# Wider weight sums in two buffers, a fold with a quarter of its own, and kept weights without padding, in a one-core encoder layer

## The chip, the core and the metric

The kernel runs on one core of a Trainium2 chip. A core has five engines that run side by side: PE multiplies matrices, DVE (VectorE) and ACT (ScalarE) work on elements, POOL (GpSimd) is a slower helper, and SP (SyncE) does nothing here but issue transfers between the chip's main memory (DRAM below) and the on-chip buffers. Each engine runs its own instructions in order. A DMA that SP issues runs on 16 DMA engines by itself; if SP has to wait before it may issue one, all that SP has behind it waits too. The metric is device time in microseconds (us), the median of three runs.

## The reference

One layer of a hybrid encoder on 2048 prompt rows and 64 sample rows of width 1024, in float32:

```
h    = rmsnorm(x, g1) * (1 + sc1) + sh1
u, q, k, v, o, gates = split(h @ w_in)
pool_out = (causal window means of u - u) @ w_pool * s_pool        # 4 channel groups
hs   = mlstm(q, k, v, gates)                                      # 4 heads, chunks, state C, n, m
x    = x + gt1 * (concat(pool_out, norm(hs) * sigmoid(o)) @ w_out)
h2   = rmsnorm(x, g2) * (1 + sc2) + sh2
a, g = split(causal_conv3(h2 @ w_up))
x    = x + gt2 * ((silu(g) * a) @ w_down)
```

The shifts, scales and gates (sh, sc, gt) are `c_act @ w_ada + b_ada`, with one vector for the prompt and one for the sample.

## The kernel before, in words

**Arithmetic.** Every float32 product is made of three matmuls on split numbers: a weight piece is loaded (tile `raw`, L390), ACT writes its high part (L411), DVE its low part (L414), and PE multiplies high by high, high by low and low by high. The same split pieces serve more than one group of rows, so after the first split they are kept in DRAM (`hl_kept`, stored by L419) and read back whole (L395) by later groups.

**Stages.** The attention part goes over four groups of rows (group 0 to 3, to about 793 us of the profile), then the feed-forward part over three groups of 704 rows. In the attention part the large products are L477 and the small ones of the recurrent heads are L1282 to L1361; `GL` holds the decay factors of a head, `kw` its weighted keys, `at` its attention scores, `st` its states after each chunk. The feed-forward products are L1572 (up) and L2015, L2138 (down); their moving operand is `hx`, made by L768 from normalised rows that were written to DRAM (`h2d`) and are loaded again (`fscr`, L802).

**Side work.** Work that isn't on the main line runs as generators: each `yield` ends a step, and the main program calls for a step of each waiting generator from time to time (`bg` lists, `drain` finishes them). Three matter here.
- `ada` (L177) makes one modulation vector out of 16 loads of `w_ada`. In group 0 the loads go to a tile with tag "w4"; DVE sums them (L208, L210), and L220 adds up over partitions.
- `fold` (L874) folds the pooling weights into the output weights: it loads two 128-row pieces of `w_out` (L878), multiplies each by `WPT` on PE (L885), lets ACT write the result over the piece, and stores it to `wo_in` (L889). Four such pairs, in group 0.
- `up_sums` (L844) prepares the feed-forward part, where the up-projection is done with sums of weight blocks: it loads the four blocks of a tile, makes four sums or differences on DVE (L863 to L867) and stores them to `wsum` (L872). It begins with group 1, and the feed-forward part loads `wsum` in place of plain weights.

**Buffers.** The tag "w4" has four buffers of [128, 4, 256], taken in turn by `ada`, `fold` and `up_sums`. The tiles of the feed-forward part, `fscr` among them, are laid over room that the attention part gives up at its end.

**Order.** The order on each engine comes out of a list scheduler that goes by data, buffers and priorities; some instructions of the side work are pinned to the order in which they are written.

## Time and profile before

| | us |
|---|---|
| median of three runs | 2185.01 (2181.26 to 2185.93) |
| span of the profiled execution | 2178.0 |
| PE busy | 2155.1 (99%) |
| DVE busy | 1631.7 (75%) |
| ACT busy | 1093.7 (50%) |
| sums of up-projection weights on DVE | from 229.5 to 758.4 |
| loads of `w_out` for the fold | from 76.7 to 112.8 |
| stores of the fold | from 92.3 to 129.3 |

The profiled execution is one run with its own time: what the profiler calls the span is 2178.0 us, and the table's first row is measured around whole runs. A row of the timeline has its start, its duration, engine, line, operation, tiles and shape, and in brackets the idle time of the engine just before it with what ended that idle time. "SPq" rows are issues: the transfer itself lands some microseconds later.

### The profile page before, as it was taken

The page shows a single profiled execution, that of the slowest core. Times are in us where ns is not written, and L with a number is a line of the kernel's source. Part 1 is how long each engine was busy: PE and PEld are TensorE (multiplying, and loading weights), DVE is VectorE, ACT ScalarE, POOL GpSimd, SP SyncE. Part 2 cuts the span into 40 slices and gives each one's busy share as a digit, 9 for nine tenths or more (in the row PEclk, how much of TensorE's full clock was granted, in tenths as well). Part 3 has the DMA queues.
Part 4 walks back from the last instruction along what each step waited for, and adds up shares of the span by engine and source line. Part 5 has one row for each costly group of instructions (what it writes and reads, how often), then busy time and mean ns, then how long its engine had stood idle before and what let it go on. Part 6 is the DMA issues. An engine that isn't in the chain of part 4 may idle for free.

```text
span 2178.0 us, 38112 instructions
## 1 busy us (share of the span) xinstructions
PE 2155.1 (99%) x13553; PEld 2041.6 (94%) x13553; DVE 1631.7 (75%) x3040; ACT 1093.7 (50%) x2181; POOL 241.6 (11%) x474
## 2 busy tenths in 40 slices
PE   8999999999999999999999999999999999999998
PEld 7888888888899999999999999999999999999998
DVE  5868668757955678797967668888886587887874
ACT  4554335234333456474736445655655364565554
POOL 0010000001000101010101121100101331111112
PEclk9999999999999999999999999999999999999999
DMA  8886997988879387788967966666668675555542
GB/s 325 327 297 226 312 312 259 310 291 273 296 263 305 130 279 255 267 306 295 349 211 257 316 244 225 237 201 215 227 220 275 217 255 183 170 179 190 172 161 81
DMA packets 297351, 539.51 MB, mean 248 GB/s; under 512 B 25760, under 2 KB 114336, under 8 KB 297160
## 3 DMA queue, kind: packets, MB, share of 16 engines
q1 hardware_dynamic: 287720, 514.75, 69.8%
q10 hardware_dynamic: 9440, 22.32, 2.6%
q8 instruction: 107, 1.75, 0.3%
q14 instruction: 84, 0.69, 0.1%
HBM read 410.98 MB, written 125.98 MB: 247 GB/s over the span
## 4 chain that ended last, share of the span: by engine, by line
PE 82%; DMA 7%; DVE 7%; issue 2%; ACT 1%; SPq 1%; POOL 0%; DVEq 0%; POOLq 0%; ACTq 0%
PE mm L1572 35%; PE mm L477 19%; PE mm L2138 12%; PE mm L2015 8%; PE mm L1117 2%; DVE wt L414 2%; DMA raw<-w_ada 1%; DMA wt<-wsum 1%; DMA hl_kept<-wt 1%; DMA wsum<-w 1%; PE m L1307 1%; PE m L1329 1%; PE m L1327 1%; PE m L1292 1%; DVE scr L250 1%
## 5 line engine op out<-in xcount | busy, mean ns | idle before, releaser
L1572 PE MATMUL mm<-hx,wt 128*128 128x352 f32 x5544 | 887.0, 321 | 3.7 <-DVE hx L768 1.9
L1572 PEld LDWEIGHTS mm<-hx,wt 128*128 128x128 f32 x5544 | 878.6, 188 | 6.8 <-DVE hx L768 2.8
L477 PE MATMUL mm<-hl,wt 128*128 128x512 f32 (+2 forms) x1920 | 386.2, 357 | 0.2 <-ACT va L250 0.2
L411 ACT ACTIVATE wt<-raw 128x512 fp32r<-128x512 f32 (+3 forms) x470 | 276.8, 597 | 185.2 <-PE mm L477 63.5
L477 PEld LDWEIGHTS mm<-hl,wt 128*128 128x128 f32 x1920 | 315.4, 189 | 48.2 <-issue 5.3
L414 DVE TENSOR_TENSOR wt<-raw,wt 128x512 fp32r<-128x512 f32 (+3 forms) x470 | 312.2, 670 | 53.2 <-ACT wt L411 52.7
L2138 PE MATMUL mm<-av,wt 128*128 128x448 f32 (+1 forms) x1632 | 262.7, 322 | 0.0
L2138 PEld LDWEIGHTS mm<-av,wt 128*128 128x128 f32 x1632 | 250.4, 188 | 11.1
L1987 DVE SCALAR_TENSOR_TENSOR x<-mm,MOD,x 128x352 f32<-128x352 f32 (+3 forms) x360 | 167.2, 503 | 79.2 <-PE mm L2138 65.7
L2015 PE MATMUL mm<-av,wt 128*128 128x352 f32 x1344 | 220.6, 323 | 1.8 <-DVE x L1987 0.7
L2015 PEld LDWEIGHTS mm<-av,wt 128*128 128x128 f32 x1344 | 215.4, 188 | 4.8 <-DVE ea L1581 2.8
L1619 ACT ACTIVATE mm<-mm 128x352 f32<-128x352 f32 x196 | 87.8, 448 | 240.0 <-PE mm L1572 184.0
L477 PE MATMUL mm<-mx,wt 128*128 128x512 f32 (+1 forms) x960 | 182.6, 352 | 0.0
L477 PEld LDWEIGHTS mm<-mx,wt 128*128 128x128 f32 x960 | 159.3, 188 | 22.5
L1550 DVE SCALAR_TENSOR_TENSOR ta<-ea,V,ta 128x704 f32<-128x704 f32 (+1 forms) x132 | 125.6, 952 | 63.2 <-ACT ta L1545 51.2
L1550 DVE SCALAR_TENSOR_TENSOR tg<-eg,V,tg 128x704 f32<-128x704 f32 (+1 forms) x132 | 125.7, 952 | 61.0 <-ACT tg L1545 58.5
L414 DVE TENSOR_TENSOR wt<-wt 128x512 fp32r<-128x512 f32 x196 | 132.7, 683 | 12.8 <-ACT wt L411 12.7
L411 ACT ACTIVATE wt<-wt 128x512 fp32r<-128x512 f32 x196 | 119.2, 622 | 43.1 <-DMA wt<-wsum 40.1
L1759 ACT ACTIVATE tg<-tg 128x704 f32<-128x704 f32 (+1 forms) x66 | 52.5, 795 | 70.5 <-DVE tg L1550 70.5
L1528 POOL COPY ea<-UC 128x2 f32<-128x2 f32 x66 | 32.8, 497 | 482.6 <-DVE ta L1550 394.0
L1117 PE MATMUL mm<-wt,hl 128*128 128x256 f32 (+1 forms) x576 | 71.3, 284 | 0.0
L1117 PEld LDWEIGHTS mm<-wt,hl 128*128 128x128 f32 x576 | 70.4, 190 | 0.8 <-issue 0.6
(304 smaller groups left out, 2188.2 us busy)
## 6 DMA issues: line engine op xcount, KB each, us to landing
wt<-wsplit SPq DMA_DIRECT2D x132, 512.0 KB, 4.2
raw<-w_up SPq DMA_DIRECT2D x198, 256.0 KB, 3.8
wt<-hl_kept SPq DMA_DIRECT2D x96, 512.0 KB, 6.0
wt<-wsum SPq DMA_DIRECT2D x132, 256.0 KB, 5.3
wsplit<-wt SPq DMA_DIRECT2D x66, 512.0 KB, 5.5
w<-w_up SPq DMA_DIRECT2D x88, 256.0 KB, 3.7
wsum<-w SPq DMA_DIRECT2D x44, 512.0 KB, 4.9
Bd<-fscr ACTq DMA_DIRECT2D x56, 352.0 KB, 4.3
```

The source lines that it names most:

```text
L411: act.activation(u.w[:, 0, :u.n], u.raw[:, :u.n], AF.Copy)
L414: dve.tensor_tensor(out=u.w[:, 1, :u.n], in0=u.raw[:, :u.n], in1=u.w[:, 0, :u.n].bitcast(F32), op=ALU.subtract)
L477: pe.matmul(ps[bi][:, :hi - lo], U[:, a, k % 4 * P:(k % 4 + 1) * P], mv[k][:, b, lo:hi], start=(at == 0 and pi == 0), stop=(k == order[-1] ...
L1117: pe.matmul(ps[ti][:n, :cols], h[4 * kh + k4][:, b, lo:lo + n], U[:, a, k4 % 2 * cols:(k4 % 2 + 1) * cols], start=(kh == 0 and k4 == 0 and ...
L1528: pool.tensor_copy(ext[:, 0:2], UC[:, f, :])
L1550: dve.scalar_tensor_tensor(out=t[:, :E], in0=ext[:, j:j + E], scalar=wc(j, f), in1=t[:, :E], op0=ALU.mult, op1=ALU.add)
L1572: pe.matmul(bk.t[:, :FH], U[:, a, kc * P:(kc + 1) * P], Bo.at(nm, kc, b), start=(first and kc == 0 and pi == 0), stop=(kc == 3 and pi == 2 ...
L1619: act.activation(to.t[:, :FH], bk.t[:, :FH], AF.Copy)
L1759: act.activation(self.tg[:, :E], self.tg[:, :E], AF.Silu)
L1987: dve.scalar_tensor_tensor(out=x3[n][:, a:b], in0=bk.t[:, a - lo:b - lo], scalar=gt2(n, s), in1=x3[n][:, a:b], op0=ALU.mult, op1=ALU.add)
L2015: pe.matmul(bk.t[:, :FH], U[:, a, c:c + P], quad.put(op, m, b), start=(first and m == 0 and pi == 0), stop=(m == 1 and pi == 2), skip_grou ...
L2138: pe.matmul(bks[i].t[:, :hi - lo], U[:, a, k % 4 * P:(k % 4 + 1) * P], av[k][:, b, lo:hi], start=(k == 0 and (a, b) == PASSES[0]), stop=(k ...
```

## The change

It has three parts.

1. `up_sums` becomes `weight_sums`. A tile is now [128, 4, 512], there are two buffers instead of four, and 22 tiles instead of 44. A load fetches whole rows of 4 KB (before: two runs of 1 KB), and a store is one DMA of 1 MB. There are 44 loads instead of 88, 22 stores instead of 44, and 88 DVE operations on 512 columns instead of 176 on 256. A tile takes seven steps; before, each half tile took four. The new function also has a branch for sums of the down-projection's weights (`dsum`), but its list holds only the up-projection's 22 tiles, so that branch never runs and those sums are made where they were before.
2. In group 0 the two buffers of tag "w4" are cut into four quarters. `ada` goes round three of them, and `fold` has the fourth alone for all of its four pairs, with one more step after each store. A load of the fold can so be issued only when the store before it has read the quarter out and landed.
3. `hl_kept` is [32, 128, 2, 512] instead of [32, 128, 2, 528], so the two halves of a row lie side by side: a store or load moves rows of 4 KB instead of two pieces of 2 KB.

```
-    hl_kept = dr.tile([32, P, 2, WN], F32, tag="hl_kept", name="hl_kept")
+    hl_kept = dr.tile([32, P, 2, 512], F32, tag="hl_kept", name="hl_kept")
...
-        def up_sums():
-            def load(f, c):
-                w = a1.tile([P, 4, 256], F32, tag="w4", name="w4", bufs=4)
-                for i in range(2):
-                    tc.keep_in_program_order(nc.sync.dma_start(out=w[:, 2 * i:2 * i + 2, :], in_=w_up[NF * i + f].rearrange(
-                        "p (h c) -> p h c", h=2)[:, :, c:c + 256]))
-                return w
-            todo = [(f, c) for f in range(NF) for c in (0, 256)]
...
+        def weight_sums():
+            pin = tc.keep_in_program_order
+            todo = list(range(NF))
+            def load():
+                if not todo:
+                    return None
+                f = todo.pop(0)
+                w = a1.tile([P, 4, 512], F32, tag="w4", name="w4", bufs=2)
+                if f < NF:
+                    for i in range(2):
+                        pin(nc.sync.dma_start(out=w[:, 2 * i:2 * i + 2], in_=w_up[NF * i + f].rearrange("p (h c) -> p h c", h=2)))
+                else:
+                    pin(nc.sync.dma_start(out=w, in_=w_quad[f - NF]))
+                return (wsum[f] if f < NF else dsum[f - NF]), w
+            nx = [load(), load()]
+            for _ in range(4):
+                yield
+            while nx[0]:
+                to, w = nx.pop(0)
+                a11, a12, a21, a22 = (w[:, i] for i in range(4))
+                pin(dve.tensor_tensor(out=a22, in0=a21, in1=a22, op=ALU.add))
+                pin(dve.tensor_tensor(out=a21, in0=a11, in1=a21, op=ALU.subtract))
+                yield
+                pin(dve.tensor_tensor(out=a11, in0=a22, in1=a11, op=ALU.subtract))
+                yield
+                pin(dve.tensor_tensor(out=a12, in0=a12, in1=a11, op=ALU.subtract))
+                pin(nc.sync.dma_start(out=to, in_=w))
+                yield
+                yield
+                nx.append(load())
+                yield
+                yield
+                yield
+        quarters = []
+        def quarter(last=False):
+            if not quarters:
+                for _ in range(2):
+                    t = a1.tile([P, 4, 512], F32, tag="w4", name="w4", bufs=2)
+                    quarters.extend([t[:, 0:2], t[:, 2:4]])
+            if last:
+                return quarters[3]
+            quarters.insert(2, quarters.pop(0))
+            return quarters[2]
         def fold():
             for n in range(0, KD, 2):
-                w = a1.tile([P, 4, 256], F32, tag="w4", name="w4", bufs=4).rearrange("p (a b) c -> p a (b c)", a=2)
+                w = quarter(True)
...
                 nc.sync.dma_start(out=wo_in[n:n + 2].rearrange("n p c -> p n c"), in_=w)
+                yield
```

The scheduler and the buffers move instructions beyond what these lines say. Three places follow. A row has the line, the operation, the tile written and the tile read (with the number of the buffer's use), the shape, and "x3" for as many equal rows. Lines from 844 on carry numbers higher by about 20 in the changed kernel.

**The fold in group 0, on SP.** Before, from the second load of `w_out` on (`w_998` and `w_1077` are the first two pairs, `w_1090` a buffer of `ada`):

```order
L878 DMA w_1077<-w_out 128x2x512
L191 DMA w_1090<-w_ada 128x512 x2
L889 DMA wo_in<-w_998 128x2x512
L390 DMA raw<-w_qkou 128x512
L419 DMA hl_kept<-wt 256x1x512
```

In the changed kernel, where `w_758` is the tile whose last quarter is the fold's:

```order
L908 DMA wo_in<-w_758 128x2x512
L191 DMA w_757<-w_ada 128x512 x4
L390 DMA raw<-w_qkou 128x512
L419 DMA hl_kept<-wt 128x1024
L897 DMA w_758<-w_out 128x2x512
L390 DMA raw<-w_qkou 128x512
```

The second load stood ahead of the first store; it now stands behind that store, four loads of `ada` and one weight piece.

**The same on PE.** Before, around the third pair's first half (`m_1273`), and then around the last half of the fourth pair (`m_1504`):

```order
L477 MATMUL mm<-hl_474,wt 128x512 x3
L477 MATMUL mm<-hl_475,wt 128x512 x2
L885 MATMUL m_1273<-w_1223,WPT 128x128 x4
L477 MATMUL mm<-hl_475,wt 128x512
L477 MATMUL mm<-hl_574,wt 128x512 x3
```

```order
L1327 MATMUL m_1485<-st_1447,q 128x129
L1329 MATMUL m_1485<-va,at 128x129
L885 MATMUL m_1504<-w_1434,WPT 128x128 x4
L220 MATMUL m_1511<-u,ones_r 32x512
L220 MATMUL m_1511<-s_778,ones_r 32x512
L220 MATMUL m_1511<-s_1086,ones_r 32x512
L220 MATMUL m_1511<-acc,ones_r 32x512
L477 MATMUL mm<-hl_575,wt 128x512 x3
```

In the changed kernel, around the second pair's first half (`m_1202`), and then around the fourth pair (`m_1581`, `m_1587`):

```order
L477 MATMUL mm<-hl_381,wt 128x512 x3
L477 MATMUL mm<-hl_474,wt 128x512 x2
L904 MATMUL m_1202<-w_758,WPT 128x128 x4
L1347 MATMUL m_1229<-SP_184,q 128x129
L1349 MATMUL m_1229<-va,at 128x129
L1347 MATMUL m_1229<-st_1193,q 128x129
L477 MATMUL mm<-hl_474,wt 128x512
```

```order
L477 MATMUL mm<-hl_475,wt 128x512 x3
L477 MATMUL mm<-hl_574,wt 128x512 x3
L477 MATMUL mm<-hl_575,wt 128x512 x3
L904 MATMUL m_1581<-w_758,WPT 128x128 x4
L904 MATMUL m_1587<-w_758,WPT 128x128 x4
L220 MATMUL m_1594<-u,ones_r 32x512
L220 MATMUL m_1594<-s_778,ones_r 32x512
L220 MATMUL m_1594<-s_1079,ones_r 32x512
```

The second pair went back to about where the third began. The fourth went behind 17 rows of three L477 each, from `hl_575` to the next but one `hl_575`, which before stood behind L220.

**Group 3, the decay factors and states of a head, on DVE.** Before, with sums of three buffers:

```order
L867 TENSOR_TENSOR w_6153<-w_6153 128x256
L863 TENSOR_TENSOR w_6595<-w_6595 128x256
L864 TENSOR_TENSOR w_6595<-w_6595 128x256
L866 TENSOR_TENSOR w_6595<-w_6595 128x256
L867 TENSOR_TENSOR w_6595<-w_6595 128x256
L250 COPY GL<-m_6621 128x20
L250 TENSOR_TENSOR at<-at,mask 128x512
L250 TENSOR_TENSOR at<-at,mask 64x64
L250 TENSOR_TENSOR kw<-m_6670,CL 128x512
L250 TENSOR_TENSOR kw<-m_6676,CL 64x128
```

In the changed kernel, first around the copy of GL, then from behind `kw` on:

```order
L871 TENSOR_TENSOR w_5882<-w_5882 128x512
L714 TENSOR_TENSOR scr<-scr 128x352
L250 COPY GL<-m_6496 128x20
L250 TENSOR_TENSOR at<-at,mask 128x512
L250 TENSOR_TENSOR at<-at,mask 64x64
L250 TENSOR_TENSOR kw<-m_6543,CL 128x512
L250 TENSOR_TENSOR kw<-m_6549,CL 64x128
```

```order
L866 TENSOR_TENSOR w_6326<-w_6326 128x512
L867 TENSOR_TENSOR w_6326<-w_6326 128x512
L250 TENSOR_TENSOR at<-at,m_6581 128x512
L250 TENSOR_TENSOR at<-at,m_6587 64x64
L869 TENSOR_TENSOR w_6326<-w_6326 128x512
L866 TENSOR_TENSOR w_6471<-w_6471 128x512
L867 TENSOR_TENSOR w_6471<-w_6471 128x512
L250 SCALAR_TENSOR_TENSOR st_6611<-SP_185,GL,m_6607 128x129
L869 TENSOR_TENSOR w_6471<-w_6471 128x512
L250 SCALAR_TENSOR_TENSOR st_6613<-st_6611,GL,m_6607 128x129
L871 TENSOR_TENSOR w_6471<-w_6471 128x512
L250 SCALAR_TENSOR_TENSOR st_6615<-st_6613,GL,m_6607 128x129
```

Four sums on `w_6595` that stood right ahead of GL are gone from there. Sums of two tiles, `w_6326` and `w_6471`, stand behind `kw`, and two of the second tile's stand between the state steps.

**The end of the attention part, on SP.** Before:

```order
L640 DMA x2d<-scr 128x576
L872 DMA wsum<-w_7382 512x1x256
L872 DMA wsum<-w_7516 512x1x256
L594 DMA scr<-xT 128x576
L390 DMA raw<-wo_in 128x512
L390 DMA raw<-w_up 128x512
L802 DMA fscr<-h2d 128x704 x4
L640 DMA x2d<-scr 128x576
```

In the changed kernel:

```order
L1441 DMA o_pool<-PO 128x120
L594 DMA scr<-xT 128x576
L390 DMA raw<-wo_in 128x512
L802 DMA fscr<-h2d 128x704 x4
L390 DMA raw<-w_out 128x512
L390 DMA raw<-wo_in 128x512
L640 DMA x2d<-scr 128x576
```

The last two stores of sums stood six and five rows ahead of the first loads of `fscr`. The last store of sums now stands 20 rows ahead of these loads, which stand behind a `scr<-xT` and one weight piece.

More of the change, by code (lines that the diff above doesn't have):

```diff
@@ L194, in load @@
                 nc.sync.dma_start(out=got[i], in_=src[i])
-        lead = 4 if first else 3
+        lead = 4 if quarter else 3
         for i in range(lead):
@@ L872, in up_sums @@
-                pin(nc.sync.dma_start(out=wsum[f, :, :, c:c + 256], in_=w))
+                yield
[9 more added lines that the diff above has]
+            return quarters[2]
```

24 lines of the change are left out of this document (6 added, 18 removed).

## The prediction

> **What bounds the kernel now.** I read the page first, then the table of busy time by stretch, then the tensor engine's timeline wherever a stretch of the touched part has idle time in it. From the page: the span, the tensor engine's row, and the engines' shares of the chain that ended last.
>
> ```profile
> span 2178.0 us, 38112 instructions
> ...
> PE 2155.1 (99%) x13553; PEld 2041.6 (94%) x13553; DVE 1631.7 (75%) x3040; ACT 1093.7 (50%) x2181; POOL 241.6 (11%) x474
> ...
> PE 82%; DMA 7%; DVE 7%; issue 2%; ACT 1%; SPq 1%; POOL 0%; DVEq 0%; POOLq 0%; ACTq 0%
> ```
>
> PE is idle for 2178.0 - 2155.1 = 22.9 us. The change removes no matmul, so a gain can only come out of that idle time, and a loss is a new wait of PE. By stretch (start and end in us, length, then busy time and count of PE, PEld, DVE, ACT, POOL, the granted clock, DMA share, GB/s):
>
> ```profile
> 50.00:100.00 50.00, 48.65 (x265) 40.53 (x264) 40.05 (x74) 28.96 (x66) 1.01 (x1) 1.00 0.88 316
> 100.00:150.00 50.00, 49.50 (x283) 40.80 (x282) 32.33 (x68) 26.36 (x67) 3.98 (x4) 1.00 0.95 347
> 600.00:650.00 50.00, 48.97 (x369) 47.42 (x369) 28.15 (x75) 18.48 (x55) 2.82 (x3) 1.00 0.79 259
> 650.00:700.00 50.00, 50.00 (x368) 45.99 (x367) 31.04 (x87) 21.45 (x70) 3.16 (x6) 1.00 0.94 307
> 793.00:804.00 11.00, 9.00 (x52) 7.84 (x51) 9.85 (x22) 6.36 (x14) 0.00 (x0) 1.00 0.58 199
> ```
>
> In 650 to 700 the transfers run at a share of 0.94 and PE is busy for all 50.00 us: it does not starve beside full DMA engines. Idle time is 1.35, 0.50, 1.03 and 2.00 us in the other four. The timeline of PE names these waits (idle time and its releaser in brackets):
>
> ```profile
> 78.16 1.13 PE L1307 MATMUL m<-va,kw 128*128 128x129 f32 x8 [1.35 <-DVE kw L250]
> ...
> 143.60 0.30 PE L538 MATMUL m<-V,scr 128*128 128x128 f32 x1 [0.50 <-DVE scr L533]
> ...
> 630.19 0.30 PE L1282 MATMUL m<-V,k 128*64 128x128 f32 x1 [1.03 <-DVE GL L250]
> ...
> 795.92 0.59 PE L1572 MATMUL mm<-hx,wt 128*128 128x352 f32 x2 [0.61 <-DVE hx L768]
> ...
> 799.07 2.49 PE L1572 MATMUL mm<-hx,wt 128*128 128x352 f32 x12 [0.82 <-DVE hx L768]
> ...
> 802.08 2.17 PE L1572 MATMUL mm<-hx,wt 128*128 128x352 f32 x12 [0.52 <-DVE hx L768]
> ```
>
> All six end on VectorE, none on a weight that is late. Together they are 4.83 us, and that is about all that this change can win.
>
> **Part 1: the weight sums.** Groups of the tile w, and from the page a VectorE addition on 512 columns:
>
> ```profile
> L863 DVE TENSOR_TENSOR w<-w x44: 404/417/426, 229.5 to 756.1; 128x256 f32<-128x256 f32 x44
> ...
> L867 DVE TENSOR_TENSOR w<-w x44: 405/418/427, 233.3 to 758.0; 128x256 f32<-128x256 f32 x44
> ```
>
> ```profile
> L414 DVE TENSOR_TENSOR wt<-wt 128x512 fp32r<-128x512 f32 x196 | 132.7, 683 | 12.8 <-ACT wt L411 12.7
> ```
>
> Before: 4 lines x 44 x 0.418 = 73.6 us of VectorE. After: 88 x 0.683 = 60.1 us. These 13.5 us are hidden: VectorE is busy for 31.04 of 50 us in the fullest stretch of the sums. Against it, one operation is 0.683 instead of 0.418 long, so a piece that PE waits for may come up to 0.27 us later behind it. PE waited for VectorE three times in the attention part, so bounds are 0 and 3 x 0.27 = 0.8; I take +0.2. The transfers move the same bytes in half as many issues; PE does not wait for them, so 0. Where the moved order matters is shown by two places.
>
> *The last group's decay factors (GL).* VectorE, PE and the issuing queue SP there:
>
> ```profile
> 622.05 0.42 DVE L867 TENSOR_TENSOR w<-w 128x256 f32<-128x256 f32 x1
> 628.25 0.42 DVE L863 TENSOR_TENSOR w<-w 128x256 f32<-128x256 f32 x1 [5.77 <-DMA w<-w_up]
> ...
> 629.97 0.17 DVE L250 COPY GL<-m 128x20 f32<-128x20 f32 x1
> ```
>
> ```profile
> 623.60 1.20 SPq L849 DMA_DIRECT2D w<-w_up  x2
> ```
>
> VectorE stands for 5.77 us before a weight load that was issued at 623.60, does four sums from 628.25, and only then copies GL, for which PE waits 1.03 us at 630.19. In the new order no sum with a pending load stands between the copy and what precedes it, so this wait goes: -1.0 (bounds 0 and -1.03). What is late next: the sums on w_6326 and w_6471 now stand behind kw and ahead of the state sums (st). Each of these loads waits for a store of the tile before it. Store and load cost, and what PE does with st:
>
> ```profile
> wt<-wsplit SPq DMA_DIRECT2D x132, 512.0 KB, 4.2
> ...
> wt<-hl_kept SPq DMA_DIRECT2D x96, 512.0 KB, 6.0
> ...
> w<-w_up SPq DMA_DIRECT2D x88, 256.0 KB, 3.7
> wsum<-w SPq DMA_DIRECT2D x44, 512.0 KB, 4.9
> ```
>
> ```profile
> 639.20 0.39 PE L1327 MATMUL m<-st,q 128*128 128x129 f32 x2
> ```
>
> The last sum of w_5882 ends near 622.5 as in the row at 622.05. SP issues its store between 622.5 and 625.5; it lands 4.9 to 6.8 us later, and the load 3.7 to 4.9 later again: between 631 and 637. PE takes st at 639.20, 638.2 once the 1.03 us are gone. Behind the load stand two sums, the first state step (some 0.4 us), a sum, and the next step: about 3 us to the second step, which PE takes 0.45 us after the first. So the load may land up to about 635.5 before PE waits: 0 to +1.8, taken +0.3 since most of the interval is free.
>
> *The start of the feed-forward part.* SP there, and the last of VectorE's hx:
>
> ```profile
> 743.87 0.43 SPq L594 DMA_DIRECT2D scr<-xT  x1
> ...
> 756.61 2.37 SPq L872 DMA_DIRECT2D wsum<-w  x2
> ...
> 763.91 1.74 SPq L802 DMA_DIRECT2D fscr<-h2d  x4
> ```
>
> ```profile
> 801.08 1.38 DVE L768 TENSOR_TENSOR hx<-fscr,hx 128x352 fp32r<-128x352 f32 x3
> ```
>
> The first loads of the normalised rows (fscr) use room that the weight sums' last stores at 756.61 free, and start at 763.91; what follows ends with hx at 801.08, and PE waits 0.61 + 0.82 + 0.52 = 1.95 us there (2.00 in the table). After, with 7 steps per tile instead of 8 per pair of half tiles, the last store stands 20 rows ahead of these loads, and the loads stand right behind the load scr<-xT that was issued at 743.87. They can start more than 10 us sooner; hx was late by under 1 us at a time. So -2.0 (bounds 0, if hx waits for VectorE's queue and not for its rows, and -2.0).
>
> **Part 2: the fold alone in one quarter.** Before, its four loads rotate over four buffers. After, each load waits until the preceding store from the same quarter has landed, and holds up what SP has behind it; between a store and the next load SP issues a few other DMAs (one, three and two weight pieces). Rows: the load's and the store's time to landing, the first store, the folds on PE, the last store, and what PE does behind the last fold.
>
> ```profile
> w<-w_out SPq DMA_DIRECT2D x4, 512.0 KB, 7.5
> ```
>
> ```profile
> DMA to landing us min/median/max: 6.8/6.8/6.8
> ```
>
> ```profile
> 92.30 0.38 SPq L889 DMA_DIRECT2D wo_in<-w  x1
> ...
> 129.29 0.38 SPq L889 DMA_DIRECT2D wo_in<-w  x1
> ```
>
> ```profile
> 107.97 1.05 PE L885 MATMUL m<-w,WPT 128*128 128x128 f32 x8
> ...
> 124.21 1.05 PE L885 MATMUL m<-w,WPT 128*128 128x128 f32 x8
> ...
> 127.58 1.06 PE L885 MATMUL m<-w,WPT 128*128 128x128 f32 x8
> ...
> 129.56 11.86 PE L477 MATMUL mm<-hl,wt 128*128 128x512 f32 x51
> ```
>
> A store follows the second half of its fold by 129.29 - 127.58 = 1.7 us. PE's new order has fold 2 just ahead of the old place of fold 3 (107.97), without the two halves of the old fold 2 ahead of it (about 0.85 us each) and three matmuls earlier (0.23 each): PE comes to it at 105.5. Fold 3 begins one matmul behind the old place of fold 4 (124.21), with one fold less ahead: 122.7. Fold 4 stands behind the 51 matmuls (0.23 each), which end at 141.4, less one fold and the four small ones that now stand behind it (129.56 - 127.58 - 0.85 = 1.1): 138.6. The second halves of folds 2 and 3 stand at 107.97 less one half and 127.58 less two, so the stores of folds 1, 2 and 3 are issued at 92.3, 108.8 and 127.6. PE covers store plus load up to 13.2, 13.9 and 11.0 us. By the rows they take 6.8 + 7.5 = 14.3: waits of 1.1, 0.4 and 3.3, in all +4.8. But those 7.5 us were measured with SP issuing without a stop; after a wait for a store the queue is nearly empty, and the nearest row for a load of 512 KB is then 4.2: 11.0 in all, and nothing waits. I take a load between (5.5): only fold 4 waits, 12.3 - 11.0 = +1.3. Bounds 0 and +4.8. What queues behind it on PE is everything; on SP the weight loads wait too, but their matmuls are those that PE runs as cover.
>
> The Trainium skill's fixed-cost rule (DMA: Bandwidth & Descriptors, Anatomy of one DMA — SWDGE (gpsimd) path: about 2.0 us plus bytes over 436 GB/s) would make 512 KB an estimated 3.2 us, store and load 6.4, and the fold's term 0, so a sum lower by 1.3; the rows of this trace are longer throughout, on another issue path, and I go by them.
>
> **Part 3: kept split weights without padding.** Stores and loads become whole rows. The nearest rows are wsplit (whole rows, 4.2) and hl_kept (padded, 6.0): up to 1.8 us sooner per load. No wait of PE above ends on such a load, so 0; the cover is that they are issued well ahead, as 650 to 700 shows.
>
> **Sum** against the profiled time: -2.0 - 1.0 + 0.3 + 0.2 + 1.3 = -1.2 us on the span of 2178.0. That span is 7.0 us below the median of 2185.01; the difference lies outside the program and is carried over: 2183.8 us.
>
> **Rivals.** (a) *More waits go*: VectorE's 13.5 us and the shorter transfers also remove the waits at 78.16 and 143.60, and the fold is free: -2.0 - 1.0 - 1.85 = -4.85, 2180.2. For it: both end on VectorE. Against: the sums are not yet running there, so VectorE's work is the same. (b) *Slower: the fold's one quarter becomes a chain* of store, load, matmul. It decides from 13.2, 13.9 and 11.0 us on. At 14.3 it costs 4.8; each further us costs three, since all three are then over: 15.3 gives +7.8. With only half of the gains (-1.5) and the other losses (+0.5): +6.8, 2191.8. For it: a DMA share of 0.95 in 100 to 150; against: SP's own wait empties the queue. The Trainium skill (Trainium Kernel Development and Optimization, Best Practices) asks for double buffers so that DMA overlaps compute, which speaks for this rival; no row of before shows the fold with one. (c) *Nothing moves*: hx is late by VectorE's own queue, GL by another operation, and the fold is covered: 2185.0. That the diff's sums of the down weights run is excluded: its list holds the 22 up-projection tiles only.
>
> **How the numbers follow.** Forecast 0.50, (a) 0.15, (b) 0.22, (c) 0.13. This kernel's runs can tell about 0.2% from no change, 4.4 us. Faster by more needs all of (a), or a good part of it and the spread of the medians: 0.16. Slower by more comes from (b) without its weakest part, and a sliver of the rest: 0.20. Same: 0.64. The range goes from (a), less 1.2 for the spread of single runs (2181.26 to 2185.93), to (b): 2179.0 to 2191.8. The forecast's own range is 2181.5 to 2187.
>
> **What would show it.** Right: no idle time of PE at 793 to 804, none before the GL matmul; at the fold PE waits once, before its fourth tile, for w<-w_out. Wrong: waits of over 1 us on w<-w_out at two or three folds (b); idle time left at the feed-forward start with fscr landed early (c); a wait of PE on st in the last group, which would be the two buffers' price mis-sized; or a changed duration of one L477 or L1572 matmul, which nothing here foresees.

## The result: about 7 us less

The changed kernel takes 2176.43 us (median of six runs, 2172.94 to 2180.3) beside 2184.27 for the kernel before (2181.26 to 2188.65). The ratio is 0.9968, 95% interval 0.9956 to 0.9980, and in a second comparison 0.9971 (0.9958 to 0.9985). Forecast were 2183.8 us in a range of 2179.0 to 2191.8: the sign was right, the size far too small, and the time lies below the range.

From the page of the changed kernel, span, PE, and the shares of the chain that ended last:

```profile
span 2172.8 us, 37945 instructions
...
PE 2154.3 (99%) x13553; PEld 2043.0 (94%) x13553; DVE 1624.5 (75%) x2952; ACT 1094.8 (50%) x2181; POOL 244.7 (11%) x474
...
PE 91%; DVE 3%; DMA 3%; issue 1%; ACT 1%; POOL 0%; SPq 0%; DVEq 0%; POOLq 0%; ACTq 0%
```

PE is idle for 18.5 us instead of 22.9. By stretch, in the same five as before:

```profile
50.00:100.00 50.00, 48.37 (x254) 39.77 (x254) 39.52 (x72) 28.13 (x65) 1.01 (x1) 1.00 0.90 310
100.00:150.00 50.00, 50.00 (x294) 41.79 (x293) 33.04 (x70) 27.03 (x68) 4.02 (x4) 1.00 0.91 336
600.00:650.00 50.00, 50.00 (x378) 48.69 (x377) 30.77 (x71) 20.16 (x59) 2.93 (x3) 1.00 0.82 293
650.00:700.00 50.00, 50.00 (x368) 45.99 (x367) 24.12 (x67) 19.92 (x66) 3.75 (x6) 1.00 0.69 228
793.00:804.00 11.00, 11.00 (x68) 11.00 (x67) 4.79 (x9) 5.66 (x11) 0.00 (x0) 1.00 0.73 239
```

The waits at 143.6, at GL near 630 and at the feed-forward start are gone. The one at 78 stays, and a small one of 0.28 us near 95.6 is new. The sums end early: the last store of a sum is issued at 671.24, and the first loads of `fscr` at 743.93 instead of 763.91.

```profile
671.24 0.32 SPq L872 DMA_DIRECT2D wsum<-w  x1
...
743.93 1.75 SPq L802 DMA_DIRECT2D fscr<-h2d  x4
```

The fold: SP's issues and PE's arrival for the second and the fourth pair, and then the landing times as far as the profile has them, of two of the four stores and of the third pair's load:

```profile
93.24 0.38 SPq L908 DMA_DIRECT2D wo_in<-w  x1
...
97.04 0.38 SPq L897 DMA_DIRECT2D w<-w_out  x1
...
128.46 0.38 SPq L908 DMA_DIRECT2D wo_in<-w  x1
...
132.01 0.44 SPq L897 DMA_DIRECT2D w<-w_out  x1
```

```profile
105.45 1.05 PE L904 MATMUL m<-w,WPT 128*128 128x128 f32 x8
...
138.93 1.95 PE L904 MATMUL m<-w,WPT 128*128 128x128 f32 x16
```

```profile
DMA to landing us min/median/max: 3.0/3.0/3.0
...
DMA to landing us min/median/max: 6.2/6.2/6.2
```

No row of the fold waits for its load. The load for the fourth pair is issued at 132.01, 3.6 us behind the store; if it takes the 6.2 us of the third pair's, it is there at an estimated 138.2, and PE comes at 138.93.

The first profiles of the two kernels differ by 5.2 us, the medians by 7.8. Why these two numbers differ has to be explained too, and so further executions of both kernels were profiled. The expectations below name their theories by letters: **A**, the gain is waits of PE on VectorE that are gone, through the order of instructions; **B**, wide transfers make PE's stream as a whole faster; later **C**, PE has two paces; **D**, VectorE stands before late loads, with PE behind it; and **E**, the wait at GL is usually longer than the first profile shows.

### The profile page after: what moved, and what is told of

Read it like the earlier page. It is cut to its first block, busy times and chain, and to the rows that moved or that the text cites. A ratio compares the mean times of both kernels' runs of the same rounds, so it can differ in the third digit from the quotient of the medians.

```text
span 2172.8 us, 37945 instructions
## 1 busy us (share of the span) xinstructions
PE 2154.3 (99%) x13553; PEld 2043.0 (94%) x13553; DVE 1624.5 (75%) x2952; ACT 1094.8 (50%) x2181; POOL 244.7 (11%) x474
## 4 chain that ended last, share of the span: by engine, by line
PE 91%; DVE 3%; DMA 3%; issue 1%; ACT 1%; POOL 0%; SPq 0%; DVEq 0%; POOLq 0%; ACTq 0%
PE mm L1592 37%; PE mm L477 24%; PE mm L2158 12%; PE mm L2035 9%; PE mm L1137 3%; DVE wt L414 1%; DMA hl_kept<-wt 1%; PE m L1327 1%; PE m L1349 1%; PE m L1347 1%; PE m L1312 1%; DMA wt<-wsum 1%; DMA wt<-dsum 0%; PE mm L1074 0%; PE m L1302 0%
## 5 line engine op out<-in xcount | busy, mean ns | idle before, releaser
L477 PE MATMUL mm<-hl,wt 128*128 128x512 f32 (+2 forms) x1920 | 386.8, 357 | 0.1
L477 PEld LDWEIGHTS mm<-hl,wt 128*128 128x128 f32 x1920 | 315.4, 189 | 48.1 <-issue 5.3
L477 PE MATMUL mm<-mx,wt 128*128 128x512 f32 (+1 forms) x960 | 183.0, 352 | 0.3 <-DVE scr L250 0.3
L477 PEld LDWEIGHTS mm<-mx,wt 128*128 128x128 f32 x960 | 159.4, 188 | 23.1 <-PE mm L477 0.5
(304 smaller groups left out, 2180.3 us busy)
```

Of the source, the lines that this page charges most:

```text
L477: pe.matmul(ps[bi][:, :hi - lo], U[:, a, k % 4 * P:(k % 4 + 1) * P], mv[k][:, b, lo:hi], start=(at == 0 and pi == 0), stop=(k == order[-1] ...
```

## Experiments

### The change again, and its parts alone

**The change itself, second profile.** No edit.

> The changed kernel as it is, beside the kernel before on one chip. The two profiled spans differ by 5.2 us (2178.0 and 2172.8), the medians by 7.8 us. Theory A (order): the gain is the waits of PE on VectorE that are gone (630, 795 to 802, 143.6, 260.6, and some later ones), so 4 to 6 us. Rival B (transfers): longer packets make PE's stream as a whole faster, which one pair of profiles may not show; then 7 us or more, with PE busy time lower by more than 2 us.

Ratio 0.9971 (0.9958 to 0.9985), span 2173.7. PE is busy for 2154.5 us, much as in the first profile of the change, and idle for 19.2. The places are those of theory A. Busy time is only 0.6 us below that of the kernel before, where B asked for more than 2. That the medians differ by 6 to 8 us remains open at this point.

**Part 1 alone: the weight sums.** The fold and `ada` go round all four quarters:

```
-            if last:
-                return quarters[3]
-            quarters.insert(2, quarters.pop(0))
-            return quarters[2]
+            quarters.append(quarters.pop(0))
+            return quarters[3]
```

`hl_kept` keeps 528 columns, and the step after the fold's store, which belongs to part 2, is left out. In this order a quarter can be filled again before the fold has used it, so the folded half of the output weights is not the reference's; instructions and bytes are those of the others.

> Only part 1: weight sums 512 columns wide in two buffers; ada and fold go round all four quarters as before, and kept rows stay padded. Theory A: waits at GL near 630 (1.03 us) and at the feed-forward start (1.95 us) are gone, the one at 143.6 (0.50 us) stays: -3 to -4 us against before. Rival B: since the sums move most of the packets that got longer, nearly the whole gain, -5 us or more.

0.9976 (0.9966 to 0.9986), 5.2 us less by the ratio and 4.6 by the medians, which lies between the two forecasts: most of the gain. GL and the feed-forward start have no wait. Nor is there one at 78 or at 143.6, where A expected the latter to stay. Against it stands one at the fold, where PE comes 6.4 us after the load's issue at 98.59 (the kernel before has 0 to 0.80 us at this place, see below):

```profile
106.99 1.13 PE L902 MATMUL m<-w,WPT 128*128 128x128 f32 x8 [2.00 <-DMA w<-w_out]
```

**Part 2 alone: the fold's own buffer.** Four buffers of [128, 4, 256] as before, the fourth for the fold only, and the step after the store; sums as before.

```
...
+            if not quarters:
+                for _ in range(4):
+                    t = a1.tile([P, 4, 256], F32, tag="w4", name="w4", bufs=4)
+                    quarters.append(t.rearrange("p (a b) c -> p a (b c)", a=2))
+            if last:
+                return quarters[3]
+            quarters.insert(2, quarters.pop(0))
+            return quarters[2]
...
```

> Only part 2: the fold has one buffer of four alone, ada goes round the other three, one more step after the store; sums and kept rows as before. Theory A: the folds' new places move ACT's and PE's work so that the wait at 143.6 goes (-0.5 to -0.7 us), with a new wait of under 0.5 us near 95; the waits at 630 and 795 to 802 stay: 0 to -1 us in all. The prediction's step (fold 4 waits for its load) says +1.3 us.

1.0007 (0.9996 to 1.0017): nothing. The fold doesn't wait for a load, and the wait at 143.6 is gone, but GL and hx are late as ever, GL by more than in any execution of the kernel before:

```profile
634.64 0.30 PE L1296 MATMUL m<-V,k 128*64 128x128 f32 x1 [2.85 <-DVE GL L250]
```

**Part 3 alone: kept weights without padding.** In the kernel before:

```
-    hl_kept = dr.tile([32, P, 2, WN], F32, tag="hl_kept", name="hl_kept")
+    hl_kept = dr.tile([32, P, 2, 512], F32, tag="hl_kept", name="hl_kept")
```

> Only part 3: kept split weights as whole rows; instruction order equal to before. Theory A: loads wt<-hl_kept land in about 4.5 instead of 6.0 us, PE waits where it waited before: 0 us (within 0.5). Rival B: -2 us or more.

1.0004 (0.9993 to 1.0016): nothing. The loads don't even land sooner, where 4.5 us had been expected: 6.0 us before, 6.0 here, and in the change:

```profile
wt<-hl_kept SPq DMA_DIRECT2D x96, 512.0 KB, 5.9
```

**The change without part 3.** The same line the other way round, in the changed kernel.

> The changed kernel with the third part undone: kept split weights padded again (528 columns), everything else and the order of all engines as in the change. Alone this part gave 1.0004 of the time before. Theory A: PE waits for no kept weight, so within 1 us of the changed kernel, 0.9965 to 0.9980 of before. Rival D: kept loads of 562 instead of 327 ns of issue on SP delay the weight-sum loads behind them, VectorE waits for these and PE for VectorE: +2 us or more against the change, with a wait on st near 638.

0.9978 (0.9967 to 0.9990): as the change, within the intervals. No wait on `st`. So the gain belongs to part 1; parts 2 and 3, each by itself, can't be told from nothing.

### What in the weight sums does it

**Eight steps per tile instead of seven.**

```
                 nx.append(load())
                 yield
                 yield
                 yield
+                yield
```

> The changed kernel with eight steps per weight-sum tile instead of seven: the last store of a sum stands 4 rows ahead of the first loads of fscr on SP, as before the change (20 with it); no sum stands ahead of GL. Theory A (order): PE's waits on hx at 795 to 802 come back, +1.5 to +2.5 us against the changed kernel, so -4 to -5 us against before. Rival B (wide transfers): those waits stay away, since 22 long stores are done sooner than 44 short ones; -6 to -7 us.

0.9974 (0.9964 to 0.9984), as the change. The last store comes late again and holds the loads of `fscr` back, as the prediction has it, yet PE loses only 0.52 us:

```profile
754.59 1.08 SPq L872 DMA_DIRECT2D wsum<-w  x1
...
760.83 1.75 SPq L802 DMA_DIRECT2D fscr<-h2d  x4
```

```profile
798.27 4.93 PE L1593 MATMUL mm<-hx,wt 128*128 128x352 f32 x28 [0.52 <-DVE hx L768]
```

They start at 760.83 instead of 763.91, but the main line is 2.3 us sooner here too: PE's first matmul on `hx` is at 791.24 instead of 793.49. Counted back from that matmul, the last of the eight loads is issued 9.8 us ahead here, 7.6 to 8.5 us ahead in the four executions of the kernel before, and 24.7 in the change; PE waits for 0.52, 1.34 to 2.70, and 0 us. So the wait goes with this lead, and a lead longer by 1 to 2 us was worth most of it; why these were won with the store back in its place is not shown. Neither theory's time for this run fitted.

This kernel also has the old pace of the sums: 22 tiles of eight steps are as many steps as 44 half tiles of four. So the gain isn't the pace.

**Short rows.** The transfers of the sums in two column halves:

```
-                        pin(nc.sync.dma_start(out=w[:, 2 * i:2 * i + 2], in_=w_up[NF * i + f].rearrange("p (h c) -> p h c", h=2)))
+                        for c in (0, 256):
+                            pin(nc.sync.dma_start(out=w[:, 2 * i:2 * i + 2, c:c + 256], in_=w_up[NF * i + f].rearrange("p (h c) -> p h c", h=2)[:, :, c:c + 256]))
...
-                pin(nc.sync.dma_start(out=to, in_=w))
+                for c in (0, 256):
+                    pin(nc.sync.dma_start(out=to[:, :, c:c + 256], in_=w[:, :, c:c + 256]))
```

> The changed kernel with each load and store of the weight sums cut into two column halves: as many DMAs, and the same short runs of 1 KB, as before the change; VectorE's operations and the steps stay those of the change. Theory A: order and width of VectorE's operations decide, so within 1 us of the changed kernel, -6 to -7 us against before. Rival B (packets): most of the gain goes, -3 us or less.

1.0037 (1.0023 to 1.0051): 8 us more than before by the ratio, 9.5 by the medians, and some 14 more than the change. Theory A as it stood falls with this: order and width on VectorE are those of the change. But it isn't B's way either. The profiled span is 13.4 us above the mean of the change's three (below): 8.6 in idle time of PE, and 4.8 in busy time, which two stretches at half clock behind its longest waits explain (last section). The two longest:

```profile
285.25 2.09 PE L1329 MATMUL m<-va,kw 128*128 128x129 f32 x8 [2.39 <-DVE kw L250]
...
648.97 0.49 PE L1349 MATMUL m<-st,q 128*128 128x129 f32 x2 [3.93 <-DVE st L250]
```

The second is the place that the prediction named as "what is late next". VectorE's first sum of the tile in question, and SP's issues of its load, here and then in the change:

```profile
647.24 0.69 DVE L867 TENSOR_TENSOR w<-w 128x512 f32<-128x512 f32 x1 [7.14 <-DMA wt<-hl_kept]
```

```profile
639.26 3.12 SPq L857 DMA_DIRECT2D w<-w_up  x4
```

```profile
629.07 0.81 SPq L856 DMA_DIRECT2D w<-w_up  x2
```

The profile puts the 7.14 us down to another load, but the last issue of the tile's own, at 641.77, landed 5.3 us later, just ahead of this sum. Counted from the copy of GL (632.42 here, 625.12 in the change), VectorE begins the tile 14.8 instead of 8.9 us later, and the state steps stand behind it. The first wait, at 285.25, comes behind loads of the modulation weights: VectorE stands for 3.19 and 2.69 us before `raw<-w_ada` at 264.20 and 272.73, and from 275.1 on it has work without a gap up to `kw`.

SP's issues of the sums' loads over the whole kernel, here and in the change (duration of one in ns: least, median, most):

```profile
L857 SPq DMA_DIRECT2D w<-w_up x88: 539/606/1502, 216.6 to 659.2; - x88
```

```profile
L856 SPq DMA_DIRECT2D w<-w_up x44: 328/424/1202, 216.9 to 642.0; - x44
```

Four issues of 0.606 us per tile instead of two of 0.424 keep SP for 2.4 instead of 0.8 us, with two stores of the same kind ahead. The run changes the length of the rows and the number of issues together, so these two aren't told apart. That two buffers leave no room for the longer issues is argued: no run has short rows with another number of buffers.

**Three steps per half tile in the kernel before.**

```
                 w = nx.pop(0)
                 yield
-                yield
```

> The kernel before with one step fewer per half tile (three instead of four) and nothing else: half tiles, four buffers, short rows. The last store of a sum stands 33 rows ahead of the loads of fscr, and no sum that waits for a load stands ahead of GL in group 3. Theory A: the waits at 630 and at 795 to 802 go, those at 78 and 143.6 stay: -3 to -5 us. Rival B: 0 to -1 us.

1.0039 (1.0024 to 1.0053), 9 us more instead of 3 to 5 less. The waits at GL and at the feed-forward start are gone as foreseen. But VectorE now waits seven times for loads of the sums, 14.6 us in all (8.7 in three before), and 40.0 instead of some 30 us for loads of modulation weights. PE waits behind it in groups 1 and 2. The longest of these waits, and what VectorE stood before just ahead of it, a modulation weight:

```profile
  DMA w<-w_up: 14.6, 7
```

```profile
454.53 0.49 PE L1328 MATMUL m<-va,at 128*128 128x129 f32 x2 [3.02 <-DVE at L250]
```

```profile
451.86 0.75 DVE L210 SCALAR_TENSOR_TENSOR s<-raw,CA,s 128x512 f32<-128x512 f32 x1 [4.63 <-DMA raw<-w_ada]
```

**Six steps per tile in the change.**

```
                 nx.append(load())
                 yield
                 yield
-                yield
```

> The changed kernel with six steps per weight-sum tile instead of seven (eight gave 0.9974, seven 0.9971 of before): the next load is asked for as long after the store as before, but its sums come one step sooner. Theory D (VectorE stands before late loads, and PE behind it): waits of VectorE on w<-w_up grow from 1.2 us to 5 or more, PE waits on kw, at, st in groups 1 to 3 for 2 to 8 us in all, 0.998 to 1.002 of before. Rival (only the two places of the prediction count): same as the change.

1.0000 (0.9989 to 1.0011): one step of seven takes the whole gain back, as theory D has it. VectorE's waits on the sums' loads are 8.9 us. PE's longest wait behind 50 us is for `kw`, and right behind it stands one for a kept weight that hadn't landed; VectorE's row shows that ahead of GL and `kw` it stood before a modulation weight:

```profile
440.02 0.91 PE L1326 MATMUL m<-va,kw 128*128 128x129 f32 x6 [2.10 <-DVE kw L250]
...
442.49 2.93 PE L477 MATMUL mm<-hl,wt 128*128 128x512 f32 x6 [1.20 <-DMA wt<-hl_kept]
```

```profile
437.78 0.75 DVE L210 SCALAR_TENSOR_TENSOR s<-raw,CA,s 128x512 f32<-128x512 f32 x1 [4.73 <-DMA raw<-w_ada]
```

The four runs together, beside all executions of the two kernels and part 1 alone (us; VectorE's waits from 200 us on, added up over the timeline; the last column is SP's time in issues of the sums' loads and stores):

| | time ratio | PE idle | VectorE waits for `w_up` | for `w_ada` | SP |
|---|---|---|---|---|---|
| before, four executions | 1 | 22.9 to 24.9 | 8.6 to 9.2 | 28.8 to 31.4 | 78 to 80 |
| change, three executions | 0.9968, 0.9971 | 18.5 to 20.2 | 1.2 to 4.8 | 11.4 to 14.5 | 28 to 29 |
| part 1 alone | 0.9976 | 21.0 | 3.5 | 14.7 | 30 |
| eight steps | 0.9974 | 18.4 | 0 | 22.1 | 25 |
| six steps | 1.0000 | 23.0 | 8.9 | 17.5 | 26 |
| short rows | 1.0037 | 27.9 | 7.1 | 25.9 | 85 |
| three steps, half tiles | 1.0039 | 29.3 | 14.6 | 40.0 | 79 |

What counts is whether the loads that VectorE's side work needs have landed when its order comes to them. Theory D speaks of the sums' own loads; those of the modulation weights, which go through SP as well, weigh more. They don't land sooner after their issue in the change (5.7 us in the median, 4.7 before), and yet VectorE waits for them half as long, so it is the issue that comes sooner, seen from VectorE. Seven or eight steps with whole rows leave time for that; six steps, or short rows, don't, and half tiles at a faster pace don't either. The sum of VectorE's waits isn't PE's price, though: what PE pays hangs on what stands behind such a wait. With eight steps VectorE stands for 7.95 us before `raw<-w_ada` at 429.53, and PE doesn't wait there.

**The change without the additional step of the fold.**

```
                 nc.sync.dma_start(out=wo_in[n:n + 2].rearrange("n p c -> p n c"), in_=w)
-                yield
```

> The changed kernel without the additional step after the fold's store: PE comes to the folds sooner (fold 2 some 6 matmuls, fold 4 14 matmuls earlier), so there is less work between a store and the matmuls on the next load. Measured in the change: a store lands in 3.0 us, a load in 6.2, and SP is 0.8 to 2.4 us late between them. Theory A: folds 3 and 4 now have 9 to 11 us of cover against 10 to 11.6 needed, so PE waits for w<-w_out 1 to 4 us in all: 0.998 to 0.9995 of before. Rival (the step is worth nothing): no wait on w<-w_out over 0.3 us, same time as the change.

0.9995 (0.9986 to 1.0003). The fold's fourth pair waits, as computed:

```profile
130.78 1.13 PE L904 MATMUL m<-w,WPT 128*128 128x128 f32 x8 [0.96 <-DMA w<-w_out]
```

The profiled execution shows 0.96 us there, 0.34 for ACT behind it, and 0.7 at the state steps near 640; by the ratios the kernel lost 5 to 6 us against the change. Beside the change without part 3, which was timed together with it, it took 2.4 us more (medians 2180.03 and 2177.63). The profiled execution was its fastest of eleven, so what the others lost isn't seen and stays open. That the step is worth something is shown, its price only roughly.

### Why the medians gain more than the first two profiles

**The kernel before, three more executions.** No edit.

> The kernel before against itself, with a profile of another execution. Time ratio 1.000. Open so far is why the medians differ by 6 to 8 us while the two first profiles differ by 5.2. Theory C (two paces): the up-projection's matmuls on 352 columns run at 158.6 or at 166.7 ns each from one wait of PE to the next; the first profile of before has 55 at the slow pace, two kernels with the old weight sums had 395 and 582 (3.2 and 4.8 us), the changed one 133 and 65. If typical executions of before hold a slow stretch, this profile's span is 2180 to 2184 with 300 or more slow matmuls. Rival (the first profile is typical): a span near 2178, under 150 slow ones, and the additional gain must come from elsewhere.

> The kernel before, a third profiled execution. So far PE's wait on GL in group 3 took 1.03 and 2.32 us in two executions of it (0.88 and 2.85 in two kernels with the same sums), and after the two long ones the granted clock fell to one half for 3.6 us (1.7 us lost). Theory E (that wait is long in many executions, and costs the half clock as well): a wait of 0.9 to 3 us, and the half clock wherever it is over 2 us; idle 22 to 25 us, span 2178 to 2187. Against it: waits under 1.1 us here and in the next look; the long ones then explain single executions only.

> As the look before: PE's wait on GL 0.9 to 3 us, half clock after it if over 2 us, idle 22 to 25 us.

Against itself the first gave 0.9998 (0.9986 to 1.0010). Its span is 2182.1 us; the other two have 2183.9 and 2179.0. The first profile, 2178.0, was the mildest of four. PE's waits on `kw` in group 1 and on GL in group 3, in the order of the three expectations:

```profile
261.85 1.13 PE L1307 MATMUL m<-va,kw 128*128 128x129 f32 x8 [0.93 <-DVE kw L250]
...
632.95 0.30 PE L1282 MATMUL m<-V,k 128*64 128x128 f32 x1 [2.32 <-DVE GL L250]
```

```profile
261.31 1.13 PE L1307 MATMUL m<-va,kw 128*128 128x129 f32 x8 [1.04 <-DVE kw L250]
...
631.73 0.30 PE L1282 MATMUL m<-V,k 128*64 128x128 f32 x1 [1.78 <-DVE GL L250]
```

```profile
260.88 1.13 PE L1307 MATMUL m<-va,kw 128*128 128x129 f32 x8 [0.82 <-DVE kw L250]
...
631.74 0.30 PE L1282 MATMUL m<-V,k 128*64 128x128 f32 x1 [2.22 <-DVE GL L250]
```

In the first profile these were 0.17 and 1.03. `kw` is late for the same kind of reason as GL: VectorE stands for 7.4 to 7.9 us in all four before a load of the modulation weights that sits ahead of GL and `kw` in its order. In the change it has no such wait there. The row is that of the second of these three executions:

```profile
259.06 0.75 DVE L210 SCALAR_TENSOR_TENSOR s<-raw,CA,s 128x512 f32<-128x512 f32 x1 [7.90 <-DMA raw<-w_ada]
```

Theory C, a slow stretch of PE in typical executions, had 77, 542 and 29 slow matmuls here: the span of 2182.1 came without one, so it is not what sets this kernel apart (below). Theory E holds for the length of the wait, but the half clock followed it in one of four executions only.

**The change, a third execution.** No edit.

> The changed kernel, a third profiled execution: no wait of PE on GL, none over 0.6 us between 100 and 790, no half clock ahead of the end, idle 18 to 20 us, span 2172 to 2176 (2172.8 and 2173.7 so far).

Span 2176.1. No wait on GL, none on hx; but the state steps waited for 1.57 us, against the expectation, behind 4.78 us of VectorE before the last-loaded tile. PE's row, and VectorE's:

```profile
639.96 0.49 PE L1347 MATMUL m<-st,q 128*128 128x129 f32 x2 [1.57 <-DVE st L250]
```

```profile
638.23 0.69 DVE L866 TENSOR_TENSOR w<-w 128x512 f32<-128x512 f32 x1 [4.78 <-DMA w<-w_up]
```

Waits of PE in us, all executions of the two kernels (w_out: at the fold; st with the two small waits behind it; idle: span less PE's busy time):

| | kw 260 | GL 630 | hx 795 to 805 | w_out | st 638 | PE idle | PE busy | span |
|---|---|---|---|---|---|---|---|---|
| before | 0.17 | 1.03 | 1.95 | 0 | 0 | 22.9 | 2155.1 | 2178.0 |
| | 0.93 | 2.32 | 1.34 | 0.80 | 0 | 24.9 | 2157.2 | 2182.1 |
| | 1.04 | 1.78 | 2.37 | 0.55 | 0 | 24.4 | 2159.5 | 2183.9 |
| | 0.82 | 2.22 | 2.70 | 0 | 0 | 24.9 | 2154.1 | 2179.0 |
| change | 0 | 0 | 0 | 0 | 0 | 18.5 | 2154.3 | 2172.8 |
| | 0 | 0 | 0 | 0 | 0 | 19.2 | 2154.5 | 2173.7 |
| | 0 | 0 | 0 | 0 | 1.87 | 20.2 | 2155.9 | 2176.1 |

Means: idle 24.3 and 19.3, busy 2156.5 and 2154.9, span 2180.8 and 2174.2, so 5.0 us of waits and 1.6 of busy time, 6.6 in all. That agrees with the ratios. Of the 5.0, the five columns give 5.0 - 0.6 = 4.4 (means 0.74 + 1.84 + 2.09 + 0.34 less 0.62); the rest is scattered over small waits, most of them in the feed-forward part. Of the 1.6, about 0.4 is the half clock in one of the four executions (last section), and the rest isn't shown to belong to the change.

### Attempts at a better version

**Two steps per piece in the first modulation vector.** In `ada`:

```
             load(i + lead)
             yield
+            if quarter:
+                yield
```

> An attempt at a better version: the change, with two steps instead of one per piece in the first modulation vector, so that fewer of its 0.74 us sums stand ahead of the first head's GL and kw on VectorE, for which PE waits 1.35 us at 78. Theory A: that wait shrinks below 0.4 us, and the sums of the vector end 20 us before they are used: 1 us less than the change, 0.9960 to 0.9972 of before. Against: the later loads of that vector meet the fold's, or the steps push the fold later; then no gain or a loss of 1 to 2 us.

0.9973 (0.9964 to 0.9982). The wait of 1.35 us at 78 is gone; in its place stand 0.43 at 98 and 0.7 at the state steps. No gain that can be told from the change.

**Both: that edit, and the eighth step per tile.**

> Attempt at a version that beats both: the change with eight steps per weight-sum tile (no sums between the state steps of group 3) and two steps per piece of the first modulation vector (no wait at 78). Apart they gave 0.9974 and 0.9973 of before beside 0.9971 of the change, each with one wait gone and another one new. If the waits gone add up: idle 16.5 to 17.5 us, 0.9960 to 0.9968 of before. If the folds, which come earlier in this order, meet their loads: a wait on w<-w_out of 0.5 to 2 us, and no gain over the change.

0.9961 (0.9947 to 0.9975), the lowest ratio of all, with idle time of 17.8 us, a little above the 16.5 to 17.5 expected. The wait of 0.52 us on `hx` is there as with eight steps alone. Of the attention part's waits behind 50 us one is left:

```profile
99.57 0.49 PE L1352 MATMUL m<-va,at 128*128 128x129 f32 x2 [0.94 <-DVE st L252]
```

It beats the kernel before; against the change the intervals overlap, so that it beats both isn't shown.

## Why the prediction was wrong

- **"That span is 7.0 us below the median; the difference lies outside the program and is carried over."** This step failed first. Only 1.7 to 1.8 us lie outside: by so much each of the changed kernel's runs is above its span (2174.56 and 2172.8). The other 5.2 of the 7.0 are a mild execution set against the median of others. They are most of the 7.4 us between the forecast 2183.8 and the measured 2176.43.
- **"About all that this change can win" is 4.83 us.** The same step, seen in the waits. I took one execution's waits for the kernel's, and it was the mildest of four: with `kw` near 260 and the fold's loads, which I left out, these places hold 5.0 us in it and 7.2 to 7.3 in each of the three others.
- **"The transfers move the same bytes in half as many issues; PE does not wait for them, so 0."** This step failed by its reasoning. PE waits for VectorE, and VectorE for loads that SP issues, the modulation weights' among them. SP's issues of the sums went from 79 to 28 us. With short rows, at the change's order, the kernel takes 8 to 9.5 us more than before instead of 7 less, so a term of some 14 us was put at nothing. How much of what remains against the kernel before is the price of two buffers, and how much that of the faster pace, no run tells apart.
- **GL, -1.0.** Place, cause and sign right; the term was mis-sized. The wait is 1.84 us in the mean, and it is gone in the change.
- **Feed-forward start, -2.0.** Right: 2.09 in the mean, none after. That the late stores hold the loads back fits the eight-step run, where a lead longer by 1 to 2 us took most of the wait away.
- **State steps behind the sums of two tiles, +0.3 (0 to 1.8).** Right as a place, and nearly as bounds: 0, 0 and 1.87. With short rows it became 3.93. This was the narrowest spot of the change.
- **Longer VectorE operations, +0.2.** Not seen. On the contrary the wait on `kw` near 260, which I left out with its 0.17 us, went: another 0.74 in the mean. I looked for what one operation adds, not for loads that VectorE stands before elsewhere.
- **The fold, +1.3 (0 to 4.8).** It didn't wait. The covers were right within 1 us: 12.2, 13.4 and 10.5 for the 13.2, 13.9 and 11.0 worked out. Wrong was the store's 6.8 us to landing, which took 3.0, while the load took 6.2 where I had 5.5. SP had stood still for 7.4 and 9.4 us ahead of the two stores whose landing is known; the 6.8 was one store of the old kernel that SP issued without a stop. "SP's own wait empties the queue" held for the store and not for the load: from 113 to 122 us, where the third pair's load ran, the DMA share is 1.03. The old order itself waited 0.55 and 0.80 us for `w_out` in two executions of four. The Trainium skill's rule (DMA: Bandwidth & Descriptors, Anatomy of one DMA — SWDGE (gpsimd) path), which is for another issue path, gave 3.2 us as an estimate for 512 KB: the store agrees with its 3.0, the load with 6.2 does not.
- **Kept rows, 0.** Right: the loads land no sooner (5.9 for 6.0 us).
- **The sum, -1.2.** In the means of the executions the terms are -2.1 (feed-forward start), -1.8 (GL), +0.6 (state steps), 0 (longer operations), -0.3 (the fold), -0.7 (`kw`, left out), -0.6 (other small waits) and -1.6 (busy time, not explained in full): -6.6 us. That the sign came out right is earned by the first two terms; the size wasn't.
- **The rivals.** (a), more waits go and the fold is free, came nearest, but not by its two waits: 143.6 is 0.50, 0, 0 and 0.12 in the four executions of before, and 78 stays. (b), the fold as a chain, needs less cover than the change has; without the fold's additional step it appears, with 0.96 us. (c) is out.

## What to carry to other kernels

Where PE is busy for 99% and waits behind an in-order VectorE, look for background work on VectorE that stands before a load: its lateness is passed on to whatever stands behind it. Here a step more or less in the background's pace, or the rows and number of its transfers, moved the time by 6 to 14 us. Look at every load that VectorE's work needs, also at those that the change doesn't touch: SP issues them all in one order. One profile gives the places of such waits, but their length depends on when transfers land; take three or four executions before a term is sized by one of them, and compare the profiled span with the spans of the timed runs before anything is carried over. A store that is followed by a load into the same buffer can be cheap where SP has stood still before it (3.0 us here); the landing time of a busy stretch (6.8) does not price it.

## What the runs showed of the hardware

**The clock halves after some waits of about 2 us.** After the wait of 2.32 us at GL in the second execution of the kernel before, the granted clock (the column ahead of the DMA share) falls to 0.50:

```profile
632.00:633.00 1.00, 0.05 (x1) 0.05 (x2) 0.97 (x4) 0.00 (x0) 0.00 (x0) 1.00 1.08 396
633.00:634.00 1.00, 1.00 (x6) 1.00 (x7) 1.00 (x3) 0.00 (x0) 0.00 (x0) 0.66 0.86 322
634.00:635.00 1.00, 1.00 (x6) 1.00 (x5) 0.96 (x4) 0.00 (x0) 0.00 (x0) 0.50 0.45 174
```

It stays there for 3.4 us, which costs 1.7. The same followed waits of 1.83 (at 78) and 2.85 us in part 2 alone, of 2.39 in the short-row kernel, and of 3.02 with three steps per half tile; behind 3.93 with short rows and behind 2.10 with 1.20 right after it with six steps the half clock lasted twice as long. It did not follow waits of 2.22 (before), 2.16 (three steps) and 2.00 (part 1 alone). The Trainium skill (TensorE: Matmul & The Clock Gate, HAM oscillation — how this bites in real kernels) asks for no idle gaps above about 3.4 us; these rows show the half clock after less. Its Part 1 says that the activity is judged in a window that runs freely; that could explain why 1.83 did and 2.22 didn't, but no run here tests it.

**Two paces of the same matmuls.** The up-projection's matmuls on 352 columns run at one of two paces for long stretches. Kept rows alone, and the first profile of the kernel before, in a stretch with the same work:

```profile
1620.00:1640.00 20.00, 20.00 (x122) 20.00 (x121) 13.66 (x20) 12.36 (x22) 1.76 (x6) 1.00 0.74 252
```

```profile
1620.00:1640.00 20.00, 20.00 (x128) 20.00 (x127) 14.65 (x22) 12.87 (x23) 1.62 (x6) 1.00 0.79 283
```

122 instead of 128 in 20 us (about 164 and 156 ns each), at a granted clock of 1.00 and without idle time. Six of eighteen profiles have this slow stretch, some 333 matmuls from about 1612 to 1668 that lose some 2.7 us, with the old sums and with the new. It starts where PE starts again after a short pause and ends with this product; what decides the pace was not found. It adds to the scatter of both kernels: one of the four executions of before has it and none of the change's three, so it is part of the 1.6 us of busy time in the means.
